# A two-layer decoder trunk on one core: one pool of PSUM banks for the feed-forward, and three changes of order

## The chip, the cores and the metric

The kernel runs on one core of a Trainium2 chip. The core has a matrix engine (TensorE, "PE" in the profile; its weight loads are listed apart as "PEld"), a vector engine (VectorE, "DVE"), a scalar engine (ScalarE, "ACT"), a general engine (GpSimd, "POOL") and a queue that issues transfers (SyncE, "SP"). Each takes its instructions in the order in which they were put into its queue, and waits on semaphores for the others. Matmul results land in PSUM, which has eight banks; a bank holds one tile of 128 x 512 float32. Tiles in PSUM and in SBUF come from pools with a fixed number of buffers, and an instruction that needs a new buffer waits until the last reader of the old one is done.

The metric is the device time of one execution in microseconds, as the median of several runs.

## The reference

The input is x with 1024 tokens of 1024 float32 values. Two layers follow, each with two gated feed-forwards around a mixer:

```python
for layer in range(DEPTH):
    f = swiglu(rmsnorm(h, ffn_pre_g[layer, 0]), ffn_w_gate[layer, 0], ffn_w_up[layer, 0], ffn_w_down[layer, 0])
    h = h + 0.5 * rmsnorm(f, ffn_post_g[layer, 0])
    m = rmsnorm(h, mix_pre_g[layer])
    ...
    h = h + rmsnorm(m, mix_post_g[layer])
    f = swiglu(rmsnorm(h, ffn_pre_g[layer, 1]), ffn_w_gate[layer, 1], ffn_w_up[layer, 1], ffn_w_down[layer, 1])
    h = h + 0.5 * rmsnorm(f, ffn_post_g[layer, 1])
```

`swiglu(x, wg, wu, wd)` is `(silu(x @ wg) * (x @ wu)) @ wd`, with 1024 inputs and 1408 (11 x 128) hidden columns. The mixer of the first layer is differential attention beside gated linear attention, that of the second stick-breaking attention; the change leaves both alone, except that their first projections follow a feed-forward. So there are four feed-forwards, here called l0 f0, l0 f1, l1 f0 and l1 f1.

## The kernel before, in words

All products are made with operands split into two parts, high and low, so that one product of float32 precision is three matmuls (`mm3`, L210 to L212: high by high, high by low, low by high). A split costs one ACT cast (the high part, L200 or L259) and one DVE subtraction (the low part, L201 or L260). The scaled splits of transposed inputs are at L203 and L204. Tokens are worked on in two halves of 512, each of four token tiles of 128.

**Gate and up** (`gu`, L273) are one level of a Strassen-Winograd scheme over token half, half of the input columns, and gate or up. A first loop over the 11 column tiles makes the gate's product of the first token half in a single bank `pa`: a first product over four k tiles (12 matmuls), a copy of it by ACT (L323, kept for later), a second product of 12 matmuls accumulated into the same bank, and the silu of that (L325). After column tile 2 the rows of the second token half are transposed (`make_raw`, L250), and with column tiles 3 to 6 DVE forms the sums that the scheme needs (`combos`, L305 to L314). A second loop over the column tiles makes the rest in the banks `pb`, `pc` and `pd` (60 matmuls a tile), with differences of weights on POOL (L343 to L346).

**Down** (`down_strassen`, L512) is the same scheme over token half, half of the first ten k tiles, and column half; the eleventh k tile is added as it is. Each product has four accumulators, one for each token tile: `da` (two products and the last k tile, 11 x 4 x 3 = 132 matmuls), `db` (60), `dc` (132), `de` (12) and `dd` (60, then a second use of 72). A product is ordered by `product` (L559): for each k tile all four token tiles, and only in the last k tile one token tile after the other. `gained` (L581, L582) reads an accumulator, squares it on ACT (L578) and multiplies it by a gain on DVE. Between the two uses of dd stand the reading of the first (L636), the norm and residual of the first token half (`epilogue`, L446 to L460) and the transposes of its normalised rows for the next stage (`make_x`, L192). After the second use come L644, the norm and residual of the second half, and, at the end of the kernel, the output.

**Buffers.** While a feed-forward runs, PSUM is divided by `open_ffn_psum` (L57) into six banks for accumulators (`acc`) and two for transposes (`tp`). Raw weights have four buffers (`rp`), split weights six (`wp`), one for each k tile of a down product; split token operands have eight (`hp`).

**Behind the feed-forward.** After l0 f0 and l1 f0 the mixer's `first_proj` (L708) projects the first token half for two column tiles (48 matmuls, `pps`), then transposes the second half's rows (`xps`) and projects them, and then closes the feed-forward's pools. After l0 f1 the next `gu` follows.

**What sets the order.** The code states a program order, but instructions are put into the engines' queues by a planner that simulates the engines with its own durations and takes, at each moment, the first instruction in program order that it believes ready. So the queues interleave work of several steps: transposes stand between matmuls of dd, and splits of weights between steps of the norm. Once a queue is made it is fixed; where the chip is slower than the planner thought, an engine waits at the instruction in front.

**Start.** Four row tiles of x are loaded and normalised (`normed`, L181 to L183); `make_x` transposes them column tile by column tile, four transposes to a bank, and splits each. A small transpose (`gps`, L98) brings the gains into columns and takes a bank of `tp`.

Of the kernel before, what the change touches and what calls it, by code (L numbers as in the profile page):

```python
# [19 lines left out]
P = 128  # L20
# [14 lines left out]

class Trunk:
# [20 lines left out]
    def open_ffn_psum(self):  # L57
        self.fctx = ExitStack()
        self.acc = self.dyn(self.fctx, "acc", 6, space=PSUM)
        self.tp = self.dyn(self.fctx, "tp", 2, space=PSUM)  # L60

    def open_fo(self):
        """row buffers of the norms"""
        self.foctx = ExitStack()
        self.fp = self.dyn(self.foctx, "fp", 4, side="right")
        self.hctx = ExitStack()
        self.hrow = self.dyn(self.hctx, "hrow", HB, side="right")

    def open_mix(self, cx, z, t, po):
        """PSUM banks of the mixers; the accumulators of the rest (self.mctx) may outlive the others"""  # L70
# [33 lines left out]
    def mixer_consts(self):  # L104
# [7 lines left out]
        # additive masks, rows q, columns k: NEG where k > q (incl) or k >= q (strict)  # L112
# [9 lines left out]
        # level masks: source row s in the even half of the block of target column t  # L122
# [13 lines left out]
        # lambda of the differential attention, on every partition  # L136
# [20 lines left out]
        # twice: the gate's first factor arrives in two parts, 16 rows each  # L157
# [85 lines left out]
    def make_raw(self, xns, gname, gi, pool):  # L243
        """gained, transposed k tiles, not split"""
# [28 lines left out]
    def gu(self, cx, wg, wu, A, xn1, gname, gi):  # L273
        """A: split k tiles of the first token half; xn1: rows of the second half.
        Returns per column tile, per token half [P, TB] = silu(gate) * up."""
# [23 lines left out]
        def combos(j):  # L299
            # S1 = A21 + A22, S3 = A11 - A21, S2 = S1 - A11, S4 = A12 - S2 (S3, then S4 in A21's place)  # L300
# [15 lines left out]
        ph = []  # L316
        for c in range(NF):
# [6 lines left out]
            self.quarter(ps, w1, A[4:8], False, True)  # L324
            nc.scalar.activation(out=h[0], in_=ps, func=AF.Silu)  # L325
# [3 lines left out]
            if 3 <= c <= 6:  # L329
                combos(c - 3)  # L330
        S[4] = [self.split(R[j], self.xp) for j in range(4)]
# [5 lines left out]
        for c in range(NF):  # L337
# [4 lines left out]
            # T1 = B12 - B11, T2 = B22 - T1, T3 = B22 - B12, T4 = B21 - T2  # L342
# [32 lines left out]
    def down_step(self, w, f0, H, f, KT, accs):  # L375
        """first column half, one K tile, all token tiles"""
# [7 lines left out]
    def down(self, w, H, pg, order=None, prep=None, mid=None, begun=None):  # L384
        """begun: accumulators of the first column half that hold all but the last K tile"""
# [38 lines left out]
    def wp_tag(self):  # L424
        class _W:
            def tile(_, shape, dt, name, tag):
                return self.wp.tile(shape, dt, name=name, tag="w")
        return _W()

# [1 line left out]
    def epilogue(self, tb, fo, ss, half, hsrc, hdst, last):  # L431
        """fo: rows [P, D], or pairs of halves"""
# [68 lines left out]
    # ---- down projection of both token halves: one level of Strassen-Winograd over  # L501
    # (token half, half of the first 2 * KH k tiles, column half); the last k tile is added as it is ----
    def down_sums(self, ph, j):
        """S1 = A21 + A22, S3 = A11 - A21 (in A21's place) of k tile j"""
# [7 lines left out]
    def down_strassen(self, w, ph, pg, hsrc, hdst, nxt):  # L512
# [10 lines left out]
        def raw(j, k=None, cols=None):  # L523
            """[P, 2, TB]: both column halves of k tile j, or a column half of the two k tiles j, k"""
# [13 lines left out]
        # B11 = (j, 0), B12 = (j, 1), B21 = (j + KH, 0), B22 = (j + KH, 1)  # L538
# [727 lines left out]
```

## Time and profile before

| | |
|---|---|
| median of three runs | 2570.22 us (2561.74 to 2572.24) |
| profiled execution | span 2559.7 us; no time of its own beside the span is listed, and the three runs lie 2.0 to 12.5 us above it |
| PE busy | 2452.2 us, 96% |
| DVE, ACT, POOL busy | 1724.8, 1071.6, 665.6 us |
| granted PE clock, mean | 0.987 |
| l0 f0: gate and up / down | 18.4 to 249.7 / 250.0 to 370.5 us |

In the profile's timeline a row holds the start in us from the span's start, the duration in us, the engine, the line, the operation, the tile written and the tiles read, the shapes, the count, and in brackets how long the engine had been idle and what ended that. In tile names the numbers are left out, so `db` is all four accumulators. Durations of matmuls overlap: the next one starts before the last has ended. In a table of stretches each engine has its busy time and, in brackets, its number of instructions. The granted clock is the share of full speed that PE was given.

### The profile page before, as it was taken

The page shows a single profiled execution, that of the slowest core. Times are in us where ns is not written, and L with a number is a line of the kernel's source. Part 1 is how long each engine was busy: PE and PEld are TensorE (multiplying, and loading weights), DVE is VectorE, ACT ScalarE, POOL GpSimd, SP SyncE. Part 2 cuts the span into 40 slices and gives each one's busy share as a digit, 9 for nine tenths or more (in the row PEclk, how much of TensorE's full clock was granted, in tenths as well). Part 3 has the DMA queues.
Part 4 walks back from the last instruction along what each step waited for, and adds up shares of the span by engine and source line. Part 5 has one row for each costly group of instructions (what it writes and reads, how often), then busy time and mean ns, then how long its engine had stood idle before and what let it go on. Part 6 is the DMA issues. An engine that isn't in the chain of part 4 may idle for free.

```text
span 2559.7 us, 32932 instructions
## 1 busy us (share of the span) xinstructions
PE 2452.2 (96%) x12253; PEld 1995.3 (78%) x12253; DVE 1724.8 (67%) x2635; ACT 1071.6 (42%) x2141; POOL 665.6 (26%) x542
## 2 busy tenths in 40 slices
PE   7999999999999999999999998999999999999997
PEld 6787777788777787887777887778888978878776
DVE  6767685754656758667789677845545476676777
ACT  6423454322545646323455234442323344642343
POOL 2445430110000001445424455300000000034543
PEclk9999999999999999999999999999999999999999
DMA  5221551112100254223452215521111034422145
GB/s 176 75 83 65 188 190 49 62 38 75 34 30 34 103 181 123 74 83 115 148 194 83 83 58 181 175 92 35 34 42 34 30 112 163 135 77 79 62 157 188
DMA packets 238841, 251.97 MB, mean 98 GB/s; under 512 B 9860, under 2 KB 186200, under 8 KB 238680
## 3 DMA queue, kind: packets, MB, share of 16 engines
q1 hardware_dynamic: 238680, 249.85, 30.0%
q8 instruction: 97, 1.59, 0.2%
q14 instruction: 64, 0.52, 0.1%
HBM read 215.21 MB, written 34.60 MB: 98 GB/s over the span
## 4 chain that ended last, share of the span: by engine, by line
PE 72%; DVE 15%; issue 4%; DMA 3%; POOL 3%; ACT 3%; SPq 0%; DVEq 0%; POOLq 0%; ACTq 0%
DVE hl L201 4%; PE z L763 4%; PE pps L210 4%; PE pps L212 4%; PE pps L211 4%; PE pd L210 3%; PE pd L211 3%; PE pd L212 3%; PE pc L211 3%; PE pc L212 3%; PE pc L210 3%; DMA rawd<-in_ffn_w_down_dram 2%; PE vps L210 2%; PE vps L211 2%; PE vps L212 2%
## 5 line engine op out<-in xcount | busy, mean ns | idle before, releaser
L172 POOL TENSOR_TENSOR rs<-ms,nhalf 128x1 f32<-128x1 f32 (+1 forms) x136 | 98.6, 732 | 1064.1 <-DVE ms L170 1007.5
L259 ACT CAST wq<-rawt 128x512 fp32r<-128x512 f32 x264 | 163.5, 622 | 340.0 <-PE pc L212 167.2
L260 DVE TENSOR_TENSOR wq<-rawt,wq 128x512 fp32r<-128x512 f32 x264 | 227.7, 866 | 46.6 <-ACT wq L259 41.0
L201 DVE TENSOR_TENSOR hl<-rawd,hl 128x512 fp32r<-128x512 f32 x200 | 162.5, 815 | 106.9 <-ACT hl L200 106.6
L200 ACT CAST hl<-rawd 128x512 fp32r<-128x512 f32 x200 | 123.6, 621 | 223.5 <-issue 60.4
L210 PE MATMUL pps<-hl,wh 128*128 128x512 f32 x512 | 208.3, 408 | 1.1 <-ACT hl L203 1.1
L212 PE MATMUL pps<-hl,wl 128*128 128x512 f32 x512 | 204.1, 399 | 0.0
L211 PE MATMUL pps<-hl,wh 128*128 128x512 f32 x512 | 204.0, 399 | 0.0
L343 POOL TENSOR_TENSOR rawt<-rawt 128x512 f32<-128x512 f32 x44 | 66.5, 1512 | 406.4 <-DMA rawt<-in_ffn_w_up_dram 243.2
L210 PE MATMUL pa<-hl,wq 128*128 128x512 f32 x352 | 140.9, 408 | 12.3 <-ACT ph L323 12.0
L210 PE MATMUL pd<-hl,wq 128*128 128x512 f32 x352 | 140.2, 398 | 10.7 <-DVE c L357 10.7
L210 PE MATMUL vps<-vh,hl 128*128 128x256 f32 x512 | 146.9, 287 | 0.0
L212 PE MATMUL vps<-vh,hl 128*128 128x256 f32 x512 | 145.0, 283 | 0.0
L211 PE MATMUL vps<-vl,hl 128*128 128x256 f32 x512 | 144.8, 283 | 0.0
L780 DVE COPY att<-tps 128x512 f32<-128x512 f32 (+2 forms) x96 | 56.3, 586 | 129.6 <-PE tps L778 129.0
L763 PE MATMUL z<-k,q 128*128 128x512 f32 (+5 forms) x444 | 139.9, 396 | 1.8 <-ACT b L796 1.0
L210 PE MATMUL pc<-hl,wq 128*128 128x512 f32 x352 | 137.7, 391 | 3.6 <-ACT hl L200 3.2
L212 PE MATMUL pa<-hl,wq 128*128 128x512 f32 x352 | 138.9, 397 | 1.6 <-DVE wq L260 1.6
L211 PE MATMUL pa<-hl,wq 128*128 128x512 f32 x352 | 140.2, 398 | 0.0
L211 PE MATMUL pd<-hl,wq 128*128 128x512 f32 x352 | 140.1, 398 | 0.0
L212 PE MATMUL pd<-hl,wq 128*128 128x512 f32 x352 | 139.7, 397 | 0.0
L212 PE MATMUL pc<-hl,wq 128*128 128x512 f32 x352 | 138.3, 393 | 0.0
(280 smaller groups left out, 6725.4 us busy)
## 6 DMA issues: line engine op xcount, KB each, us to landing
rawt<-in_ffn_w_gate_dram SPq DMA_DIRECT2D x88, 512.0 KB, 3.7
rawd<-in_ffn_w_down_dram SPq DMA_DIRECT2D x60, 512.0 KB, 3.6
rawd<-in_ffn_w_down_dram SPq DMA_DIRECT2D x116, 256.0 KB, 2.6
rawt<-in_ffn_w_up_dram SPq DMA_DIRECT2D x44, 512.0 KB, 3.8
hres<-h SPq DMA_DIRECT2D x40, 512.0 KB, 2.9
h<-hres SPq DMA_DIRECT2D x40, 512.0 KB, 5.0
rawt<-in_hyb_w_in_dram SPq DMA_DIRECT2D x16, 512.0 KB, 3.9
rawt<-in_sb_w_qkv_dram SPq DMA_DIRECT2D x16, 512.0 KB, 3.8
```

The costliest lines, as they stand in the source:

```text
L172: nc.gpsimd.tensor_tensor(out=rs, in0=ms, in1=self.nhalf.to_broadcast([P, n]) if n > 1 else self.nhalf, op=ALU.pow)
L200: nc.scalar.copy(out=t[:, 0], in_=src)
L201: nc.vector.tensor_tensor(out=t[:, 1], in0=src, in1=t[:, 0].bitcast(F32), op=ALU.subtract)
L210: nc.tensor.matmul(ps, lhsT=ah, rhs=bh, start=first, stop=False, skip_group_check=more)
L211: nc.tensor.matmul(ps, lhsT=ah, rhs=bl, start=False, stop=False, skip_group_check=more)
L212: nc.tensor.matmul(ps, lhsT=al, rhs=bh, start=False, stop=last, skip_group_check=more)
L259: nc.scalar.copy(out=w[:, 0], in_=src)
L260: nc.vector.tensor_tensor(out=w[:, 1], in0=src, in1=w[:, 0].bitcast(F32), op=ALU.subtract)
L343: gt(out=b11, in0=b12, in1=b11, op=ALU.subtract)
L763: nc.tensor.matmul(z[:, :wide], lhsT=lhs[:, i * P:(i + 1) * P], rhs=rhs[:, c0:c0 + wide], start=j == 0, stop=j == len(passes) - 1 and not ...
L780: (nc.scalar.copy if j0 else nc.vector.tensor_copy)(out=t[:, :n], in_=ps[:, :n])
```

## The change

Four things change in the feed-forward; no arithmetic does.

1. PSUM is one pool of eight banks, from which accumulators and transposes take alike.
2. In the first loop of `gu` the second product of a column tile is issued after the first product of the next column tile (`a12`).
3. `product` takes the last k tile as a part of the same call (`more`), so its operands are split with the others before the matmuls; and the second use of dd gets `tail=KH + 1` = 6, which makes the order "for each token tile all six k tiles" in place of "for each k tile all four token tiles". For the other products the order of matmuls stays as it was.
4. The first transposes of the kernel (`make_first_x`) run token tile by token tile into eight banks, and the splits follow.

```diff
+class Tagged:
+    def __init__(self, pool, tag):
+        self.pool, self.tag = pool, tag
+
+    def tile(self, shape, dtype, name, tag=None):
+        return self.pool().tile(shape, dtype, name=name, tag=self.tag)
...
     def open_ffn_psum(self):
         self.fctx = ExitStack()
-        self.acc = self.dyn(self.fctx, "acc", 6, space=PSUM)
-        self.tp = self.dyn(self.fctx, "tp", 2, space=PSUM)
+        self.acc = self.dyn(self.fctx, "acc", 8, space=PSUM)
+        self.tp = Tagged(lambda: self.acc, "acc")
...
+    def make_first_x(self, xns, gname, gi, pool):
+        ps = [self.tp.tile([P, TB], F32, name="xps") for k in range(KD)]
+        for t in range(NTT):
+            for k in range(KD):
+                self.nc.tensor.transpose(ps[k][:, t * P:(t + 1) * P], xns[t][:, k * P:(k + 1) * P], self.ident)
+        return [self.split(ps[k], pool, scale=self.col(gname, gi * KD + k)) for k in range(KD)]
...
+        second = []
+
+        def a12():
+            ps, w1, h = second.pop()
+            self.quarter(ps, w1, A[4:8], False, True)
+            nc.scalar.activation(out=h[0], in_=ps, func=AF.Silu)
+
         for c in range(NF):
...
             self.quarter(ps, w0, A[0:4], True, True)
             nc.scalar.copy(out=h[1], in_=ps)
-            self.quarter(ps, w1, A[4:8], False, True)
-            nc.scalar.activation(out=h[0], in_=ps, func=AF.Silu)
+            if second:
+                a12()
+            second.append((ps, w1, h))
             ph.append(h)
...
+        a12()
         S[4] = [self.split(R[j], self.xp) for j in range(4)]
...
-        def product(accs, a, b, start, ks=range(KH)):
+        def product(accs, a, b, start, ks=range(KH), more=None, tail=TAIL):
             As, Bs = [], []
-            for j in ks:
-                As.append(self.split(a(j), self.hp))
-                Bs.append(self.split(b(j), wp))
+            for a, b, ks in [(a, b, ks)] + ([more] if more else []):
+                for j in ks:
+                    As.append(self.split(a(j), self.hp))
+                    Bs.append(self.split(b(j), wp))
             n = len(As)
-            m = max(0, n - TAIL)
+            m = max(0, n - tail)
...
-        product(pa, A(0, 1), lambda j: half(j + KH, 0), False)
-        product(pa, *last_k(0, 0))
+        product(pa, A(0, 1), lambda j: half(j + KH, 0), False, more=last_k(0, 0))
...
-        product(pd, A(1, 1), t4, False)
-        product(pd, *last_k(1, 0))
+        product(pd, A(1, 1), t4, False, more=last_k(1, 0), tail=KH + 1)
...
-        x0 = self.make_x(self.xn0, "ffn_pre_g", 0, self.xp)
+        x0 = self.make_first_x(self.xn0, "ffn_pre_g", 0, self.xp)
```

More of the change, by code (lines that the diff above doesn't have):

```diff
@@ L424, in wp_tag @@
     def wp_tag(self):
[L425 to L428, printed above, removed]
+        return Tagged(lambda: self.wp, "w")
     def epilogue(self, tb, fo, ss, half, hsrc, hdst, last):
@@ L584, in down_strassen @@
         A = lambda tb, kh: (lambda j: ph[j + kh * KH][tb])
-        last_k = lambda tb, c: (lambda j: ph[NF - 1][tb], lambda j: half(NF - 1, c), False, [0])
+        last_k = lambda tb, c: (lambda j: ph[NF - 1][tb], lambda j: half(NF - 1, c), [0])
         s1 = lambda j: self.s1[j]
@@ L617, in down_strassen @@
             tt(out=c22[t], in0=pc[t], in1=u2[t], op=ALU.add)
-        product(pc, A(0, 1), lambda j: half(j + KH, 1), False)
-        product(pc, *last_k(0, 1))
+        product(pc, A(0, 1), lambda j: half(j + KH, 1), False, more=last_k(0, 1))
         for t in range(NTT):
@@ L625, in down_strassen @@
         pe = new("de")
-        a, b, _, ks = last_k(1, 1)
+        a, b, ks = last_k(1, 1)
         product(pe, a, b, True, ks)
```

## The prediction

> **What bounds the kernel now.** I read the engine totals and the chain of waits first, then the waits of TensorE, then stretches and timelines around each long wait.
>
> ```profile
> PE 2452.2 (96%) x12253; PEld 1995.3 (78%) x12253; DVE 1724.8 (67%) x2635; ACT 1071.6 (42%) x2141; POOL 665.6 (26%) x542
> ...
> PE 72%; DVE 15%; issue 4%; DMA 3%; POOL 3%; ACT 3%; SPq 0%; DVEq 0%; POOLq 0%; ACTq 0%
> ```
>
> TensorE is the bound almost everywhere: time can only come from its idle stretches and from the ends of the kernel, where it has nothing to do. Its longest waits (total, times, longest):
>
> ```profile
> PE db L210 <- DVE fo L582: 15.6, 4, 4.6
> PE pa L210 <- ACT ph L323: 12.0, 5, 4.0
> ...
> PE xps L192 <- DVE ms L170: 7.1, 13, 1.5
> PE xps L192 <- DVE xn L183: 6.5, 4, 2.4
> PE dd L210 <- DVE fo L636: 3.6, 7, 1.4
> ...
> PE dd L210 <- DVE c L629: 1.5, 3, 0.6
> ```
>
> The change touches all six. The next view is a table of stretches; its columns are width, busy time and count of PE, of PE's weight loads, of DVE, ACT and POOL, then PE's granted clock, DMA share and rate. First the db product in the four feed-forwards, from its first matmul to the first one of dc, and for comparison dc with de, which runs without a wait.
>
> ```profile
> 279.90:300.00 20.10, 15.49 (x62) 12.33 (x60) 15.21 (x20) 9.26 (x20) 8.57 (x6) 0.92 0.47 167
> 1225.10:1245.10 20.00, 16.43 (x61) 13.05 (x60) 14.12 (x18) 9.27 (x20) 8.05 (x6) 0.83 0.40 143
> 1573.70:1593.20 19.50, 15.47 (x61) 12.27 (x60) 14.76 (x18) 9.27 (x20) 8.46 (x6) 0.91 0.41 151
> 2464.70:2482.00 17.30, 13.93 (x62) 11.19 (x60) 14.94 (x19) 9.27 (x20) 7.83 (x6) 1.00 0.45 158
> 300.00:329.90 29.90, 29.90 (x133) 24.77 (x132) 20.46 (x31) 12.91 (x23) 8.94 (x7) 1.00 0.42 141
> ```
>
> A matmul of 512 columns, issued without a gap, costs 29.90 / 132 = 0.2265 us (the printed mean of 0.39 us overlaps the next one). The granted clock under 1.00 shows a second cost of idling: stretches of half speed behind the wait. The next two rows are such a pair in the first feed-forward: an idle stretch, then eight matmuls in 3.50 us, 1.7 us more than 8 x 0.2265.
>
> ```profile
> 74.00:78.40 4.40, 0.44 (x2) 0.01 (x1) 4.40 (x9) 2.77 (x6) 0.00 (x0) 1.00 0.00 0
> 78.40:81.90 3.50, 3.50 (x8) 2.75 (x9) 3.50 (x7) 1.09 (x2) 0.00 (x0) 0.51 0.52 150
> 332.60:371.00 38.40, 35.50 (x163) 26.89 (x162) 34.95 (x58) 21.14 (x43) 10.74 (x11) 1.00 0.62 200
> 382.00:395.00 13.00, 7.06 (x25) 4.74 (x24) 7.84 (x13) 5.66 (x10) 3.71 (x5) 0.64 0.21 84
> ...
> 2546.20:2559.70 13.50, 0.00 (x0) 0.00 (x0) 9.10 (x22) 1.67 (x6) 2.29 (x4) 0.63 0.42 157
> ```
>
> The other three are the two products of dd in the first feed-forward, the start of the mixer behind it, and the end of the kernel after the last matmul. They are used below.
>
> **The change part by part.** No instruction of compute is added or taken away; what changes is which bank a tile gets and the order asked for.
>
> *Eight banks: db.* The timeline of the first db product:
>
> ```profile
> 280.58 0.39 PE L210 MATMUL db<-hl 128*128 128x512 f32 x1
> ...
> 282.16 1.54 DVE L201 TENSOR_TENSOR hl<-t,hl 128x512 fp32r<-128x512 f32 x1
> ...
> 285.29 1.87 DVE L582 TENSOR_TENSOR fo<-da,pg 128x512 f32<-128x512 f32 x3
> ...
> 286.02 0.50 PE L210 MATMUL db<-hl 128*128 128x512 f32 x1 [4.61 <-DVE fo L582]
> ```
>
> Token tiles 0 and 1 of db get the two banks that da leaves; tile 2 waits until DVE has read da at L582. With eight banks db has four of its own. The four stretches hold 20.10 + 20.00 + 19.50 + 17.30 = 76.9 us; 4 x 60 matmuls at 0.2265 are 54.4; the difference, half clock included, is 22.5. What is late next are the split weights of db: its fifth and last ends at 282.16 + 1.54 = 283.7, and db wants it at 279.9 + 4 x 12 x 0.2265 = 290.8. So nothing takes the wait's place: I take **22**, with 17.9 as lower end (the busy DVE as bound, below) and 22.5 as upper.
>
> *The later second gate product.* The order of the queues at the long wait for L323:
>
> ```profile
> 70.22 1.74 POOL L345 TENSOR_TENSOR rawt<-rawt 128x512 f32<-128x512 f32 x1
> ...
> 70.72 1.78 DVE L201 TENSOR_TENSOR hl<-s,hl 128x512 fp32r<-128x512 f32 x1
> ...
> 74.13 0.68 DVE L305 TENSOR_TENSOR s<-xr 128x512 f32<-128x512 f32 x1
> ...
> 74.84 0.62 ACT L200 CAST hl<-s 128x512 fp32r<-128x512 f32 x1 [5.67 <-DVE s L305]
> ...
> 77.77 0.58 ACT L323 COPY ph<-pa 128x512 f32<-128x512 f32 x1
> ...
> 78.40 0.73 PE L210 MATMUL pa<-hl,wq 128*128 128x512 f32 x1 [3.96 <-ACT ph L323]
> ```
>
> DVE's element-wise rows take 1.78 instead of 0.68 us while POOL works, ACT stands behind DVE, and the copy of the first product stands behind that in ACT's queue. The second product of the tile cannot accumulate into the bank before the copy. In the new order the second product of the tile before, 12 matmuls or 2.7 us, lies between: a wait of 3.96 becomes about 1.2. Three long waits lose 2.7 each, 8.2; the two short ones (12.0 less three of about 3.8) some 0.6; three half-clock stretches of 1.7 go if the rest is short, 5.1. Sum 13.9; I take **13**. Upper end 17 (12.0 + 5.1); lower end -3, if the queue's next item, a weight split by the same busy DVE, is what PE then waits for, and the split held a tile longer in the six weight slots costs a little (0.7 per feed-forward).
>
> *The last down product tile by tile.* dd is used twice; its second use now includes the last k tile and asks for token tile 0 over all six k tiles, then tile 1, and so on. Three effects:
>
> (a) The waits for L636 and L629 (5.1 in all) fall away but for the first tile's: **+3** (0 to 5).
>
> (b) Tile 0 needs all six operand pairs at once. In the first feed-forward the second use began at 347.28, and the last pairs came late from DVE:
>
> ```profile
> 347.28 0.47 PE L210 MATMUL dd<-hl 128*128 128x512 f32 x1 [0.39 <-DVE fo L636]
> ...
> 350.84 0.50 PE L210 MATMUL dd<-hl 128*128 128x512 f32 x1 [0.34 <-DVE fo L636]
> ...
> 356.37 0.68 DVE L201 TENSOR_TENSOR hl<-rawd,hl 128x512 fp32r<-128x512 f32 x1
> ...
> 356.53 0.41 PE L192 MATMUL xps<-ident,fo 128*128 128x128 f32 x2 [1.08 <-DVE ms L170]
> ...
> 360.08 0.68 DVE L201 TENSOR_TENSOR hl<-rawd,hl 128x512 fp32r<-128x512 f32 x1
> ```
>
> The fifth pair is there at 357.05, the sixth at 360.76. Taken strictly, tile 0 would leave PE idle from 350 to 357 and again to 360.8, some 9 us after the transposes that fit in. Not strictly, as the transposes placed between dd's matmuls in these rows show that the planner fills, tiles 1 to 3 use the ready pairs and nothing is lost. I take 1 us per feed-forward, **-4** (-32 to 0), nearer the filling that the rows show.
>
> (c) The chains behind the product start earlier. Two lead into a mixer, where PE has 48 matmuls (11 us) left and then waits for normalised rows; with the L170 and L183 waits (7.1 + 6.5) and half clock (0.64 in 382:395) that is some 14.5 in all. A tile's chain costs DVE about 4 us (add, gain, two residual halves, normalisation), and in 332.6:371 DVE is busy 34.95 of 38.40: room for about one tile of three. So 4 per mixer, **+8** (0 to 14.5). Behind the feed-forward that leads into another one: **+1** (0 to 2.5). At the end of the kernel 13.5 us pass after the last matmul, with DVE work for all four tiles in them:
>
> ```profile
> 2537.91 0.68 DVE L201 TENSOR_TENSOR hl<-rawd,hl 128x512 fp32r<-128x512 f32 x1
> ...
> 2544.15 2.05 DVE L644 TENSOR_TENSOR fo<-dd,u 128x512 f32<-128x512 f32 x3 [5.56 <-PE dd L212]
> ```
>
> DVE has 5.56 us of free time before it, and that is the most that can move: **+4** (2 to 5.5).
>
> *The first transposes token tile by token tile.* Rows of the start:
>
> ```profile
> 10.28 0.69 PE L192 MATMUL xps<-ident,fx 128*128 128x128 f32 x2
> ...
> 12.01 0.75 DVE L183 TENSOR_SCALAR fx<-fx,rs 128x1024 f32<-128x1024 f32 x1 [0.45 <-POOL rs L172]
> ...
> 13.58 1.11 PE L192 MATMUL xps<-ident,fx 128*128 128x128 f32 x4 [0.29 <-DVE gcol L101]
> ...
> 18.41 0.78 PE L210 MATMUL pa<-hl,wq 128*128 128x512 f32 x1
> ...
> 20.83 0.60 PE L192 MATMUL xps<-ident,fx 128*128 128x128 f32 x4
> ```
>
> At 18.41 half of the 32 transposes are done; the rest come between matmuls. Now 24 can run before the fourth row tile is there (12.76). At the early pace, 1.11 for four of which the last overlaps (0.21 each), 32 from 10.3 end at 17.1: 1.3 earlier, with 16 transposes more behind them, which later cost about 0.09 each, 1.4. Together 2.7; I take **+2.5** (0 to 4.5; -1 if the eight banks, one of which holds the gains' transpose, block the first product).
>
> [...]
>
> **Sum:** 22 + 13 + 3 - 4 + 8 + 1 + 4 + 2.5 = 49.5 us less. The profiled execution has a span of 2559.7; the three runs take 2561.7 to 2572.2, so 2 to 12.5 lie around it. Against the median: 2570.2 - 49.5 = 2520.7, say **2521**. About 0.5% (13 us) is what a measurement can tell from no change.
>
> **The rivals.**
>
> *The waits move to DVE* (for: DVE is busy 15.21 of 20.10 us in db's stretch and 4.40 of 4.40 before L323; against: the weights of db are split seven microseconds ahead). Then db lasts as long as DVE's work in it, saving 4.9 + 5.9 + 4.7 + 2.4 = 17.9, and the gate's 13 is nil: 32.4 in all, **2538**.
>
> *The common pool does not deliver* (for: eight transposed tiles and four dd accumulators do not fit eight banks if these are handed out in turn; against: each bank is free again after one ACT and one DVE read, 0.69 + 0.75). Half of the transposed tiles would wait for dd, 4 x (0.69 + 0.75) or 5.8 us later, at three transitions: 17 lost, **2538** too.
>
> *The starved last product* is the slower side: PE takes the order strictly. 9 idle, 1.7 at half clock, and 3 for the next stage's weights, since all six slots are held into the last token tile: 13.7 in three feed-forwards. The last one ends at 2546.2, so its second use begins 72 x 0.2265 before, at 2529.9; five pairs take 3.4, and the sixth is there at 2538.6: 5.3 idle and 1.7. That is 48; if the sixth load comes late too, by a load, a subtraction and a split (5.2), 69. The gains outside (22 + 13 + 3 + 2.5 = 40.5) are used up at 10.1 per feed-forward; it is measurably slower from 13.3. Midway: 2570 + 18 = **2588**. For: the rows of (b). Against: the transposes between.
>
> [...]
>
> *Everything is hidden*: db 22.5, gate 17, dd 4, no starving, mixers 14.5, 2.5, end 5.5, start 2.5: 68.5, **2502**.
>
> **How the numbers follow.** Forecast 0.45, DVE 0.22, pool 0.10, all hidden 0.18, starved 0.05. The forecast's own bounds, with terms that miss independently, are about 2507 to 2540. The range takes in the two cases of 2538 and their spread and nearly all of the hidden one: 2497 to 2550, leaving out the starved case and tails. Faster by over 0.5% in nearly all but the starved case; with something for a planner that reorders every queue: 0.88 faster, 0.08 within, 0.04 slower.
>
> **What would show it.** db's stretch at 13.6 to 14 us with clock 1.00 and no wait for L582; the wait for L323 under 1.5; L644's first row several microseconds ahead of the last matmul and fewer than 10 us behind it; the first pa near 17; dd's second use no longer than 24 us. Wrong: waits of dd for L201, of pa for L260, or of pps and pa for weights behind dd.

## The result and the profile after

The changed kernel takes **2507.86 us** in the median of 4 runs (2504.94 to 2509.04), beside 2570.07 us for the kernel before (4 runs, 2561.74 to 2572.24): a ratio of 0.9771, 95% interval 0.9755 to 0.9786. The forecast was 2521 in a range of 2497 to 2550. The profiled execution took 2509.04 us with a span of 2507.3; that of before, with its span of 2559.7, fits the run of 2561.74. So the sum of 49.5 us is to be held against 52.4 between two profiled executions, and 62 between the medians. One run of one kernel below took 2680.57 us at a granted clock of 0.848, where that kernel's other three runs have 0.996 and 0.997; it is left out of that kernel's median.

The page of the changed kernel: engine totals, then the shares of the chain of waits.

```profile
PE 2430.2 (97%) x12253; PEld 1995.7 (80%) x12253; DVE 1733.3 (69%) x2635; ACT 1069.0 (43%) x2143; POOL 671.2 (27%) x542
...
PE 82%; DVE 10%; issue 3%; POOL 2%; ACT 2%; DMA 2%; DVEq 0%; SPq 0%; POOLq 0%; ACTq 0%
```

The number of matmuls is the same. PE's busy time fell by 22 us with the same instructions, so that they ran faster (mean granted clock 0.987 before, 0.994 after); the other 30 us were idle time. In the chain PE's share rose from 72 to 82%, DVE's fell from 15 to 10%. The waits of PE after (total, times, longest):

```profile
PE pd L228 <- DVE c L385: 10.7, 4, 2.7
...
PE xps L210 <- DVE xn L193: 4.3, 5, 1.7
PE pa L230 <- DVE wq L278: 4.1, 2, 3.2
PE dd L228 <- DVE fo L662: 3.9, 4, 1.3
...
PE pa L228 <- DVE hl L222: 3.4, 1, 3.4
...
PE xps L210 <- DVE ms L180: 2.8, 9, 0.5
PE dd L229 <- DVE hl L219: 2.7, 3, 0.9
PE xps L201 <- DVE gcol L111: 2.7, 1, 2.7
...
PE dd L228 <- ACT hl L218: 1.3, 1, 1.3
...
PE pa L228 <- ACT ph L349: 0.7, 1, 0.7
```

The two waits at the head of before's list are gone: 15.6 us of db for the reading of da to nothing, 12.0 us of `pa` for the copy (now L349) to 0.7. New, or longer than before, are `pa` for a weight split (L278; 1.6 us before), dd for late operands (L219, L218), and two waits at the start of the kernel (L111, L222). The longest, `pd` for L385, was in the kernel before too; it lies in the up loops and the prediction did not look at it. The stretches that answer to those of before: db in the four feed-forwards, dc with de, dd, 13 us in the first mixer from 11.3 us behind its first product on (as 382:395 before), and the end.

```profile
276.90:290.50 13.60, 13.60 (x62) 11.27 (x61) 13.46 (x16) 9.08 (x20) 8.50 (x6) 1.00 0.59 210
1202.00:1215.60 13.60, 13.60 (x62) 11.26 (x61) 11.76 (x15) 8.50 (x20) 8.52 (x6) 1.00 0.56 192
1544.90:1558.50 13.60, 13.60 (x62) 11.27 (x61) 13.46 (x16) 9.07 (x20) 7.63 (x6) 1.00 0.53 182
2418.70:2432.30 13.60, 13.60 (x62) 11.27 (x61) 13.46 (x18) 8.74 (x20) 7.30 (x5) 1.00 0.50 174
290.50:320.40 29.90, 29.90 (x133) 24.77 (x132) 21.66 (x34) 13.05 (x23) 9.08 (x7) 1.00 0.45 150
323.10:361.40 38.30, 35.49 (x165) 27.37 (x164) 35.55 (x62) 20.88 (x43) 10.68 (x11) 1.00 0.55 174
372.70:385.70 13.00, 11.04 (x62) 9.18 (x63) 9.89 (x15) 7.67 (x14) 3.67 (x4) 1.00 0.32 105
2497.70:2507.30 9.60, 0.00 (x0) 0.00 (x0) 4.77 (x11) 0.72 (x2) 1.10 (x2) 0.63 0.42 158
```

db is 13.60 us four times, with PE busy in all of it. The stretch in the mixer has 62 matmuls and transposes at full clock where before's had 25 at 0.64. Behind the last matmul DVE has 4.77 us of work left, not 9.10.

For the whole ledger I cut both traces at the first matmul of each stage; a "gate" runs from the first `pa` to the first `pc`, an "up" from there to the first da, a mixer from its first `pps` to the first `dps` of the output projection. Sums over the feed-forwards, in us:

| stage | before | after | difference |
|---|---|---|---|
| start of the span to the first product | 18.4 | 22.7 | +4.3 |
| four gate loops (77.4, 73.2, 71.7, 72.9) | 295.2 | 276.2 (70.1, 66.1, 73.9, 66.1) | -19.0 |
| four up loops | 617.4 | 615.7 | -1.7 |
| db | 77.0 | 54.4 | -22.6 |
| dd (the last one to its last matmul) | 147.1 | 148.2 | +1.1 |
| mixers (474.0, 427.2) | 901.2 | 888.0 (466.3, 421.7) | -13.2 |
| output projections (123.1, 116.1) | 239.2 | 241.1 (124.0, 117.1) | +1.9 |
| behind the last matmul's start | 14.0 | 10.0 | -4.0 |

That is 53.2 less; the products not listed give back the rest, to 52.4.

### The profile page after: what moved, and what is told of

Read it like the earlier page. It is cut to its first block, busy times and chain, and to the rows that moved or that the text cites. A ratio compares the mean times of both kernels' runs of the same rounds, so it can differ in the third digit from the quotient of the medians.

```text
span 2507.3 us, 32918 instructions
## 1 busy us (share of the span) xinstructions
PE 2430.2 (97%) x12253; PEld 1995.7 (80%) x12253; DVE 1733.3 (69%) x2635; ACT 1069.0 (43%) x2143; POOL 671.2 (27%) x542
## 4 chain that ended last, share of the span: by engine, by line
PE 82%; DVE 10%; issue 3%; POOL 2%; ACT 2%; DMA 2%; DVEq 0%; SPq 0%; POOLq 0%; ACTq 0%
PE z L788 4%; PE pps L228 4%; PE pps L230 4%; PE pps L229 4%; PE pd L228 3%; PE pd L230 3%; PE pd L229 3%; PE pa L230 3%; PE pa L228 3%; PE pa L229 3%; PE pc L229 3%; PE pc L230 3%; PE pc L228 3%; PE vps L228 3%; PE po L831 2%
## 5 line engine op out<-in xcount | busy, mean ns | idle before, releaser
L182 POOL TENSOR_TENSOR rs<-ms,nhalf 128x1 f32<-128x1 f32 (+1 forms) x136 | 100.2, 743 | 1046.1 <-DVE ms L180 950.4
L278 DVE TENSOR_TENSOR wq<-rawt,wq 128x512 fp32r<-128x512 f32 x264 | 242.8, 924 | 22.6 <-ACT wq L277 16.7
L219 DVE TENSOR_TENSOR hl<-rawd,hl 128x512 fp32r<-128x512 f32 x200 | 166.2, 834 | 86.6 <-ACT hl L218 86.3
L218 ACT CAST hl<-rawd 128x512 fp32r<-128x512 f32 x200 | 123.7, 621 | 208.5 <-issue 46.7
L371 POOL TENSOR_TENSOR rawt<-rawt 128x512 f32<-128x512 f32 x44 | 72.0, 1636 | 395.9 <-DMA rawt<-in_ffn_w_up_dram 184.9
L228 PE MATMUL pd<-hl,wq 128*128 128x512 f32 x352 | 139.9, 397 | 10.7 <-DVE c L385 10.7
L228 PE MATMUL pa<-hl,wq 128*128 128x512 f32 x352 | 138.7, 394 | 4.1 <-DVE hl L222 3.4
L230 PE MATMUL pa<-hl,wq 128*128 128x512 f32 x352 | 138.1, 393 | 4.1 <-DVE wq L278 4.1
L228 PE MATMUL pc<-hl,wq 128*128 128x512 f32 x352 | 137.6, 391 | 3.1 <-ACT hl L218 3.1
L230 PE MATMUL pc<-hl,wq 128*128 128x512 f32 x352 | 138.3, 393 | 0.0
L229 PE MATMUL pc<-hl,wq 128*128 128x512 f32 x352 | 138.3, 393 | 0.0
```

The source lines that it names most:

```text
L182: nc.gpsimd.tensor_tensor(out=rs, in0=ms, in1=self.nhalf.to_broadcast([P, n]) if n > 1 else self.nhalf, op=ALU.pow)
L218: nc.scalar.copy(out=t[:, 0], in_=src)
L219: nc.vector.tensor_tensor(out=t[:, 1], in0=src, in1=t[:, 0].bitcast(F32), op=ALU.subtract)
L228: nc.tensor.matmul(ps, lhsT=ah, rhs=bh, start=first, stop=False, skip_group_check=more)
L229: nc.tensor.matmul(ps, lhsT=ah, rhs=bl, start=False, stop=False, skip_group_check=more)
L230: nc.tensor.matmul(ps, lhsT=al, rhs=bh, start=False, stop=last, skip_group_check=more)
```

## The experiments

Each edit makes the planner put all queues together anew, so small differences far from an edit are not the edit's own. All times are medians beside the kernel before on the same chip (2562.96 to 2566.72 us there); "span" is the profiled execution's.

**One part taken out, or one part alone.** The eight banks alone, in the kernel before:

```diff
-        self.acc = self.dyn(self.fctx, "acc", 6, space=PSUM)
-        self.tp = self.dyn(self.fctx, "tp", 2, space=PSUM)
+        self.acc = self.dyn(self.fctx, "acc", 8, space=PSUM)
+        self.tp = Tagged(lambda: self.acc, "acc")
```

> The kernel before with one change: PSUM of the feed-forward as one pool of eight banks. Theory A (the wait of db for L582 is a lack of banks and nothing else, and the shorter starts of the mixers come from the token-tile order of the last product): the four db stretches go from 76.9 to 54.4 us, nothing else moves by more than 2, span 2559.7 - 22.5 = 2537. Rival B (more banks for transposes shorten the mixers' starts too, 7.7 + 5.6 us in the changed kernel): span about 2524. Both would allow the output projections, whose pools are opened by the same function, to be 1 us longer each.

Measured: 2532.22 us, ratio 0.9877 (0.9860 to 0.9893), span 2532.9. db is 13.6 four times, so this part carries its 22.6 alone. The mixers shorten too, by 5.3 and 4.3 us, without any tile order, as the rival had it. But the third gate loop gets longer, from 71.7 to 77.3, which neither case foresaw, so the span lies between the two expected. In the list of PE's waits:

```profile
PE xps L258 <- DVE xn L191: 7.3, 1, 7.3
```

With banks free, the planner put the transposes of the second token half early into PE's queue, where they waited 7.3 us for their normalised rows, with the gate's matmuls behind them.

The changed kernel without the tile order:

```diff
-        product(pd, A(1, 1), t4, False, more=last_k(1, 0), tail=KH + 1)
+        product(pd, A(1, 1), t4, False, more=last_k(1, 0))
```

> The changed kernel with the second use of dd in the old order (all four token tiles for each k tile). Theory A (the token-tile order is what shortened the mixers' starts by 13.3 us and the end by 3.9, and it costs 2.2 in the gate loop behind the feed-forward that leads into another): span 2507.3 + 13.3 + 3.9 - 2.2 - 0.6 = 2522. Rival B (the eight banks shortened the mixers' starts): the end alone is lost and the gate loop gets its 2.2 back, span about 2509.

Measured: 2512.41 us, 0.9801 (0.9786 to 0.9815), span 2511.2. The end takes 14.0 us again; the mixers lose only 0.8 and 1.6. The third gate loop does not get back the 2.2 us that both cases expected: it takes 75.1, beside 73.9 in the changed kernel. The kernel before with the tile order alone (`more` and `tail=KH + 1` as in the change):

> The kernel before (six and two banks) with only the last product changed: the last k tile in the same call, and the second use of dd token tile by token tile. Theory A (with two banks for transposes an earlier chain does not help the mixers' starts; the order gives the end of the kernel and costs about 1 us in each dd): end 10 instead of 14, mixers within 2 each, span 2559.7 - 4 to -1, about 2556. Rival B (as predicted, the chain behind dd sets the mixers' starts, and the order shortens them by 4 each whatever the banks): span about 2548.

Measured: 2563.77 us, 0.9994 (0.9979 to 1.0009), span 2564.7. The end is 4.1 us shorter (9.9) and the mixers 2.9 and 1.6, but the third gate loop is 7.6 longer (79.3). The db stretches, whose order the edit leaves alone, take 81.3 instead of 77.0. In the whole this part moves nothing that can be measured.

The changed kernel without the deferred product, where `a12()` follows each first product at once:

```diff
-            if second:
-                a12()
             second.append((ps, w1, h))
+            a12()
...
-        a12()
```

> The changed kernel with the second gate product of a tile issued straight after its first. Theory A (the deferred product covers ACT's late copy): the waits of pa for L349 come back, about 3.9 us with 1.7 of half clock in three feed-forwards, span 2507.3 + 17 = 2524. Rival B (these waits ended because the planner made another order with eight banks): no such wait, span 2507 within 3.

Measured: 2535.39 us, 0.9893 (0.9879 to 0.9908), span 2532.8. The gate loops are 76.1, 72.7, 80.8 and 74.0, together 27.4 more than in the changed kernel (17 were expected for the whole kernel), and the wait for the copy is back:

```profile
PE pa L228 <- ACT ph L349: 13.4, 6, 3.6
```

The deferred product alone in the kernel before:

> The kernel before with only the second gate product issued after the first of the next tile. Theory A (the deferral works by itself: a gate loop behind finished inputs runs at 66 us instead of 73): gate loops of l0 f1 and l1 f1 66, about 6 less in the other two, span 2559.7 - 26 = 2534. Rival B (it needs the eight banks, since two pa banks live at a time beside pb to pd): gate loops above 69, span 2545 or more.

Measured: 2544.19 us, 0.9918 (0.9894 to 0.9943), span 2542.9. Gate loops 73.8, 66.7, 69.6, 66.7: 18.4 less than before. The other two gave 3.6 and 2.1 where 6 each were expected, and db takes 81.8 here, so the span lies 9 us above the expectation. The second and fourth are near what their work takes: 276 matmuls at 0.2265 us are 62.5, and 32 transposes at some 0.11 (in the changed kernel's third gate loop they start 0.109 us apart from 1309.27 on) are 3.5, together 66.0 by this estimate.

The changed kernel with the first transposes as before (`make_x`):

```diff
-        x0 = self.make_first_x(self.xn0, "ffn_pre_g", 0, self.xp)
+        x0 = self.make_x(self.xn0, "ffn_pre_g", 0, self.xp)
```

> The changed kernel with the first transposes column tile by column tile, as before. Theory A (the token-tile order of the first transposes is a loss here: one bank is held by the gains' transpose, PE waits 2.7 us for it and the first product starts at 22.7 instead of 18.4): first product at about 18, span 2507.3 - 5 = 2502. Rival B (the later start is made up in the first gate loop, where DVE and ACT and not PE set the pace): first product at 18, but span 2507 within 1.5.

Measured: **2500.55 us**, 0.9762 (0.9747 to 0.9776), span 2498.8: 8.5 us less than the changed kernel's span. The first product starts at 18.6 instead of 22.7, and the first gate loop takes 68.1 instead of 70.1. So this part of the change costs 6.1 us at the start of the kernel. That the whole time falls with it is less sure: the ratios to the kernel before, 0.9762 here and 0.9771 for the changed kernel, are not apart.

**Why the first transposes lose.** Two causes were to be told apart: the bank that the gains' transpose holds, and DVE's queue. The changed kernel's start, from the timelines of PE and of DVE (start, duration, engine, line, operation, tiles, count, idle time before and what ended it):

```profile
14.04 5.18 PE L201 MATMUL xps<-ident,fx 128*128 128x128 f32 x25 [2.68 <-DVE gcol L111]
22.66 0.79 PE L228 MATMUL pa<-hl,wq 128*128 128x512 f32 x1 [3.43 <-DVE hl L222]
```

```profile
20.54 0.20 DVE L144 CAST lm<-lmf 128x64 int32<-128x64 f32 x1 [1.69 <-POOL lmf L141]
20.65 1.29 DVE L278 TENSOR_TENSOR wq<-rawt,wq 128x512 fp32r<-128x512 f32 x2
21.85 2.72 DVE L222 SCALAR_TENSOR_TENSOR hl<-xps,gcol,hl 128x512 fp32r<-128x512 f32 x4
```

The 25 transposes wait for the bank until 14.04 and are through at 19.22. Then DVE waits at the last of seven casts of masks (one for each entry of `LEVELS`), which POOL is still making for a mixer that starts 340 us later; the weight split and the first split of x stand behind it. The first experiment gets round the bank: the eighth column tile is transposed last.

```diff
-        for t in range(NTT):
-            for k in range(KD):
+        for t, k in [(t, k) for t in range(NTT) for k in range(KD - 1)] + [(t, KD - 1) for t in range(NTT)]:
```

> The changed kernel with the eighth column tile of the first transposes put behind the other seven, so that the bank held by the gains' transpose stops nothing. Theory A (the held bank makes the late start): 28 transposes run as the row tiles come, first product at about 20, span 2507.3 - 3 = 2504. Rival B (DVE's first splits stand in its queue behind casts of masks that wait for POOL, until 20.65): first product still at 22 to 23, span 2507 within 1.5.

Measured: 2507.89 us, 0.9778 (0.9754 to 0.9801), span 2504.0. The rows of PE and DVE:

```profile
10.71 5.98 PE L200 MATMUL xps<-ident,fx 128*128 128x128 f32 x32
22.39 0.80 PE L227 MATMUL pa<-hl,wq 128*128 128x512 f32 x1 [5.70 <-DVE hl L221]
```

```profile
12.21 0.75 DVE L193 TENSOR_SCALAR fx<-fx,rs 128x1024 f32<-128x1024 f32 x1 [0.45 <-POOL rs L182]
...
20.27 0.20 DVE L144 CAST lm<-lmf 128x64 int32<-128x64 f32 x1 [1.69 <-POOL lmf L141]
20.38 1.29 DVE L277 TENSOR_TENSOR wq<-rawt,wq 128x512 fp32r<-128x512 f32 x2
21.59 2.72 DVE L221 SCALAR_TENSOR_TENSOR hl<-xps,gcol,hl 128x512 fp32r<-128x512 f32 x4
```

All 32 transposes are done at 16.7, and the product starts no earlier than 22.39. With the casts where they were, the bank was not what set the start. Then, on top of this, the casts go to POOL:

```diff
-            nc.vector.tensor_copy(out=mi, in_=m)
+            nc.gpsimd.tensor_copy(out=mi, in_=m)
```

> The changed kernel with two edits: the gains' transpose finds a free bank (the first transposes make the eighth column tile last), and the six casts of the masks lm run on GpSimd instead of VectorE. If the first product starts at 22.7 us because the second halves of the splits stand behind these casts in VectorE's queue, while the casts wait for GpSimd's affine_selects, the first product starts between 16.5 and 19 us and the span is 2497 to 2502 us, median about 2503. If the cold transposes and the arrival of the last row tile set the start, it stays at 22 to 23 us and the span at 2504 to 2508, as with the first edit alone (22.4 us, 2504.0).

Measured: 2500.63 us, 0.9756 (0.9739 to 0.9774), span 2498.6.

```profile
15.76 1.42 PE L200 MATMUL xps<-ident,fx 128*128 128x128 f32 x11 [1.17 <-DVE fx L193]
18.02 0.50 PE L227 MATMUL pa<-hl,wq 128*128 128x512 f32 x1 [0.84 <-DVE hl L221]
```

```profile
14.95 0.75 DVE L193 TENSOR_SCALAR fx<-fx,rs 128x1024 f32<-128x1024 f32 x1 [1.70 <-POOL rs L182]
...
15.98 1.32 DVE L277 TENSOR_TENSOR wq<-rawt,wq 128x512 fp32r<-128x512 f32 x2
17.23 5.34 DVE L221 SCALAR_TENSOR_TENSOR hl<-xps,gcol,hl 128x512 fp32r<-128x512 f32 x8
```

The weight split moves from 20.38 to 15.98 and the first product from 22.39 to 18.02, by the casts alone. DVE's queue was the cause. Even so this kernel is no faster than the one with the old order (2498.6 and 2498.8). But that does not settle what the new order is worth, for the edit has a price of its own: POOL also makes a factor of each row tile's normalisation (`rs`, L182), and with the casts in its queue the last row tile is normalised at 15.7 instead of 13.0 (the L193 rows), so the first splits of x, eight of 0.67 us on DVE, cannot begin before. The new order with the casts on neither of these queues was not run.

**The third gate loop.** It is the one behind another feed-forward, and the only one that the change made longer (71.7 to 73.9). If its transposes wait for late rows, they can be asked for a column tile later (with the first transposes as before):

```diff
-            if c == 2:
+            if c == 3:
...
-            if 3 <= c <= 6:
-                combos(c - 3)
+            if 4 <= c <= 7:
+                combos(c - 4)
```

> The changed kernel with the old first transposes (as old_first_x) and with the second token half's transposes and sums one column tile later in the gate loop. Theory A (the gate loop of l1 f0 loses its 7 us because PE meets the transposes of rows that are not yet normalised): that loop 67 instead of 72.8, the others unchanged, span 2498.8 - 5 = 2494. Rival B (the loss is DVE's, which has the norm's chain and the weight splits at once; later sums then come too late for the second loop): that loop still above 71 or the second loops longer, span 2498 or more.

Measured: 2507.14 us in three runs, 0.9772 (0.9744 to 0.9799), span 2503.2. The third gate loop is 72.5 beside 72.8 with the first transposes as before, and the up loops get a new wait, of `pc` for L383, 5.5 us in four. So it is not the transposes. The wait is at the front of the loop; the changed kernel, PE and DVE:

```profile
1294.01 0.50 PE L230 MATMUL pa<-hl,wq 128*128 128x512 f32 x1 [3.19 <-DVE wq L278]
```

```profile
1288.63 0.69 DVE L278 TENSOR_TENSOR wq<-rawt,wq 128x512 fp32r<-128x512 f32 x1
...
1290.49 2.74 DVE L480 SCALAR_TENSOR_TENSOR h<-fo,rs,h 128x512 f32<-128x512 f32 x4
...
1293.27 0.69 DVE L278 TENSOR_TENSOR wq<-rawt,wq 128x512 fp32r<-128x512 f32 x1
```

Between two weight splits of the new loop DVE does the residual sums of the last token tiles (L480), and PE waits for the second. The order of the rows shows this; no run here took the norm's chain away from DVE.

**What the banks give to the mixers.** Beside the kernel with old first transposes, six banks and two again:

```diff
-        self.acc = self.dyn(self.fctx, "acc", 8, space=PSUM)
-        self.tp = Tagged(lambda: self.acc, "acc")
+        self.acc = self.dyn(self.fctx, "acc", 6, space=PSUM)
+        self.tp = self.dyn(self.fctx, "tp", 2, space=PSUM)
```

> The changed kernel with the first transposes as before, and with the banks parted again into 6 for accumulators and 2 for transposes in the feed-forward; the deferred gate product and the tile order stay. Beside the same kernel with eight banks in one pool (span 2498.8): the db stretches go back from 13.6 to about 20 us each, +25; the output projections give 1.9 back. If the eight banks also made the mixers' starts shorter, these grow by 4 to 9 us and the span is 2526 to 2531, median about 2530. If the tile order made them shorter, as predicted before the result, they stay and the span is about 2522, median about 2524.

Measured: 2540.24 us, 0.9912 (0.9890 to 0.9934), span 2537.8, which is 39.0 more: db 24.9, mixers 4.7 and 3.4, gate loops 5.4, output projections 1.8 less. The mixers answer to the banks, as in the kernel with the banks alone. The gate loops, and 2.0 us in the up loops, I had not put into the expectation, so the span came out 7 us above it. How the banks act is seen where the second token half enters the first mixer. The kernel before, PE and ACT:

```profile
389.16 0.69 PE L192 MATMUL xps<-ident,xn 128*128 128x128 f32 x2 [2.40 <-DVE xn L183]
391.43 1.05 PE L192 MATMUL xps<-ident,xn 128*128 128x128 f32 x4
...
398.73 0.61 PE L192 MATMUL xps<-ident,xn 128*128 128x128 f32 x4
```

```profile
389.67 1.27 ACT L203 ACTIVATE hl<-xps,gcol 128x512 fp32r<-128x512 f32 x2 [4.21 <-PE xps L192]
...
399.38 0.69 ACT L203 ACTIVATE hl<-xps,gcol 128x512 fp32r<-128x512 f32 x1 [0.22 <-PE xps L192]
```

With two banks, only two column tiles could be begun ahead of the last row tile, 6 transposes of 32 (that tile's first transposes start at 389.16); the other six column tiles follow one by one as ACT and DVE hand banks back, and the last split starts at 399.38. The changed kernel:

```profile
373.33 1.72 PE L210 MATMUL xps<-ident,xn 128*128 128x128 f32 x14 [0.84 <-DVE xn L193]
375.44 0.77 PE L210 MATMUL xps<-ident,xn 128*128 128x128 f32 x5 [0.40 <-DVE xn L193]
376.89 1.64 PE L210 MATMUL xps<-ident,xn 128*128 128x128 f32 x13 [0.68 <-DVE xn L193]
```

```profile
377.25 4.74 ACT L221 ACTIVATE hl<-xps,gcol 128x512 fp32r<-128x512 f32 x8 [2.53 <-PE xps L210]
```

19 of 32 transposes are done ahead of the last rows, and all eight splits run as one row of 4.74 us, done 5.1 us after the last rows' first transposes instead of 10.9.

The banks and the tile order do not do the same. Over the first 35 us of each mixer, the waits of `xps` sum to 8.9 us in the kernel before, and the granted clock is 0.85 and 0.90. The tile order alone takes the waits to 4.1, but the clock only to 0.90 and 0.95. The banks alone leave 5.7 us of waits, but the clock is 1.00 in both. The changed kernel has 4.3 and 1.00.

**The wait left in every kernel.** `pd` for L385 and `pc` for a split stand at the end of each up loop, 13.9 us in all. The kernel with old first transposes, DVE:

```profile
231.58 4.05 DVE L219 TENSOR_TENSOR hl<-ph,hl 128x512 fp32r<-128x512 f32 x3
235.55 0.68 DVE L385 TENSOR_TENSOR c<-pd,c 128x512 f32<-128x512 f32 x1
```

Splits for the down product stand ahead of the add that reads `pd`, and PE's next product accumulates into `pd`. In the last column tile the two products get banks of their own:

```diff
+            if c == NF - 1:
+                pc2 = self.acc.tile([P, TB], F32, name="pc2", tag="acc")
+                pd2 = self.acc.tile([P, TB], F32, name="pd2", tag="acc")
+                tt(out=c21, in0=pc, in1=u2, op=ALU.add)
+                self.quarter(pc2, w4, A22, True, True)
+                tt(out=c21, in0=pc2, in1=c21, op=ALU.add)
...
+                tt(out=c12, in0=pd, in1=u2, op=ALU.add)
+                self.quarter(pd2, w3, S[4], True, True)
+                tt(out=c12, in0=pd2, in1=c12, op=ALU.add)
```

> The changed kernel with the first transposes as before, and in the last column tile of the second up loop the two last products get banks of their own, so that TensorE does not wait for VectorE to add the earlier contents; the sums are made by two more adds per block. Beside the same kernel without this edit (span 2498.8): the waits of pd for c (10.7 us) and of pc for hl (3.2 us) lie there. If they are a matter of banks alone, they go, with the stretches at half clock behind them: 12 to 20 us, span 2479 to 2487, median about 2485. If VectorE's backlog of splits for the down products is what is late, the wait moves to the first products of da or db, and the gain is under 4 us, span 2495 to 2499.

Measured: **2489.00 us** (2487.46 to 2492.47), 0.9710 (0.9693 to 0.9728), span 2485.7, the best kernel here. The first up loop without and with the edit:

```profile
86.60:240.80 154.20, 150.74 (x649) 122.69 (x648) 111.73 (x138) 45.48 (x73) 79.78 (x54) 0.99 0.26 74
```

```profile
86.60:235.20 148.60, 148.60 (x649) 121.68 (x648) 107.72 (x135) 44.90 (x72) 74.88 (x51) 1.00 0.26 75
```

All four up loops are 148.6 with no wait, 20.4 us less in sum; 7.3 come back later, most of it in dc with de (0.8 to 1.2 each in three), dd (1.6) and the second mixer (2.5).

Last, on top of this, half of the tile order:

```diff
-        product(pd, A(1, 1), t4, False, more=last_k(1, 0), tail=KH + 1)
+        product(pd, A(1, 1), t4, False, more=last_k(1, 0), tail=3)
```

> The kernel with own banks at the end of the up loops (span 2485.7), and in it the last down product goes token tile by token tile over its last 3 pieces of K instead of all 6. If the order over all 6 pieces costs the third gate loop its 3 to 4 us (73.3 us, beside 69.6 in the kernel with the deferred product alone) because the last token tile's sums, norms and weight splits crowd on VectorE, and costs the waits for late operands in dd (5.4 us in four stages), then half of the order gives back part of both: third gate loop 70 to 72, dd stages 1 to 3 us shorter in sum, the end 10.0 to 12, span 2480 to 2485. If these 3 us come from the schedule of the deferred product and not from the order, the third gate loop stays at 73 to 74 and only the end moves, to 11 to 13: span 2485 to 2489.

Measured: 2489.96 us, 0.9717 (0.9699 to 0.9735), span 2487.0. The third gate loop is 72.0 (from 73.3), the last dd 0.9 shorter, the end 12.1 (from 10.0), and a mixer 1.0 longer. The direction fits the crowding on DVE; the gain expected of it did not come, and 1.3 us of one gate loop settle nothing. Why the deferred product alone has 69.6 there stays open.

## Why the prediction was right, and where not

The time fell inside the range, 13 us below the forecast. That the sum of 49.5 comes so near to 52.4 is luck: two terms were too small, two had the wrong sign, and a cost was missing.

- **db, 22 (17.9 to 22.5).** Right: 22.6, in the changed kernel and with the banks alone. DVE was busy 13.46 of 13.60 us in it and still held nothing up: the split weights were ahead, as worked out.
- **The later gate product, 13 (-3 to 17).** The mechanism was right, the size too small: 19.0 in the ledger, 18.4 alone, 25.5 in the span when it is taken out of the changed kernel. The step that failed is "the second product of the tile before, 12 matmuls or 2.7 us, lies between". By the code two products lie between a copy's bank being filled and its next use: the second of the tile before and the first of the tile after, 24 matmuls or 5.4 us. That covers the longest wait of 4.0 whole, where I left 1.2 of it; what remains is 0.7 us once. The rest was not in the list of waits at all: of the 7.0 us that the second gate loop lost, the long wait (3.61) and the half clock with it (3.41 us at 0.50) are 5.3, and the others are delays of at most 0.2 us between single matmuls, too short to be listed. The loops behind a mixer reach the 66 us that their work takes (66.1 each).
- **(a) and (b), +3 and -4.** Together right: dd +1.1 in the ledger. One by one, not as told: the waits for L636 (L662 now) did not fall (3.6 in seven, 3.9 in four; L629's 1.5 are gone), and late operands cost 2.7 + 1.3 = 4.0, the 4 foreseen. dd's second use takes 23.6 us in the first feed-forward (24 was the bound given).
- **(c) mixers, +8 (0 to 14.5).** 13.2: inside the range, but mostly for another reason. The step that failed is "The chains behind the product start earlier", with 4 for each mixer: that is the tile order, which gives 4.5 in both together when alone and 2.4 when it is taken out last; the eight banks give 9.6 alone and 8.1. The prediction read the waits of `xps` for DVE as late rows, and did not ask how many of the eight column tiles could be transposed ahead of them. It also put all 13.6 us of the two lines into the mixers; 8.6 stand there, and the rest at transposes in the dd stages and at the start.
- **+1 into the next feed-forward.** Wrong in sign: the third gate loop is 2.2 longer. PE waits 3.2 us there for a weight split (`pa` for L278), with a stretch at half clock behind it (0.50 from 1295.30 to 1302.10), as the rival has it in which the waits move to DVE. What puts the split there is open: the loop is longer with the banks alone (77.3) and with the tile order alone (79.3), but no shorter without the tile order (75.1).
- **End, +4 (2 to 5.5).** Right: 4.0 in the changed kernel, 4.1 alone, with DVE's work behind the last matmul down from 9.10 to 4.77.
- **First transposes, +2.5 (-1 to 4.5).** Wrong in sign: 6.1 us lost at the start (4.1 + 2.0). The step that failed took PE's transposes as what sets the first product. That all 32 keep the early 0.21 us, as the term has it, no run shows: with the bank free they start 0.11 apart from 15.4 on. They were done at 16.7 there, near the 17.1 of the sum, but the product started at 22.39: DVE's queue set it, and there the splits had come to stand behind casts that wait for POOL. In the old order the first splits stand between these casts.
- **Not in the sum:** 0.9 to 1.2 us for each output projection, in every kernel with eight banks there and in none without. No row shows an added wait of that size, and the cause was not tried.

The rivals: db did not last as long as DVE; the pool delivers, four db stretches and the mixers show it; PE was not starved: in the first feed-forward the last operand of dd's second use was split at 351.12, and by then PE had begun 40 of the 72 matmuls, where the strict order allows 15. The median lies nearer to "everything is hidden" (2502) than its chance says, and not because everything was hidden: the terms were read in before's fastest run and taken from its median. The profiled run of before is 8.3 us faster than the median of its runs, and that is most of the difference between 52.4 and 62.

## What to carry to other kernels

Ask of a wait for a bank how many tiles could have been ready ahead of the late operand: here the pool of eight gave two to three times as much in the mixers as the tile order from which that gain was expected. Work that has no hurry (masks for a later stage) should not stand in the queue of an engine whose next item starts the kernel; moved to another queue, it can hold up what stands there. And look at the longest wait that a change does not touch: 10.7 us of `pd`, in plain sight in every list, was worth more than two of the four parts of the change, for a bank of its own to each of two products.

## What the runs showed of the hardware

**The pace of the first transposes.** In the kernel that goes round the bank, nothing but transposes has run on PE (after the gains' one) when the first two of these stretches follow each other:

```profile
10.70:15.40 4.70, 4.70 (x23) 4.69 (x23) 2.53 (x10) 1.14 (x2) 2.80 (x10) 1.00 1.00 285
15.40:16.50 1.10, 1.10 (x12) 1.05 (x10) 0.20 (x1) 0.86 (x2) 0.71 (x3) 1.00 1.16 294
...
22.35:25.60 3.25, 3.21 (x8) 2.55 (x9) 3.25 (x6) 0.00 (x0) 0.00 (x0) 0.50 0.81 266
```

Up to 15.4 the transposes start 0.21 us apart (22 in 4.70 us), from then on 0.11 (the other ten in 1.10). In the changed kernel the run of 25 that begins at 14.04 has its starts 0.213 apart up to 18.58 and 0.11 from 18.74 on, 4.6 us into the run and 3.9 us ahead of the first matmul of `pa`. In the kernel before, eight transposes follow the wait of 1.67 us that ends at 16.37, and `pa`'s first matmul starts 2.0 us later; its matmuls start 0.43 apart from 18.99 to 20.27, and the four transposes from 20.83 on 0.11. The prediction took the early 0.21 for all 32; in the two kernels above the pace rose ahead of the first matmul. (The granted clock reads 1.00 in both of the first rows and so does not tell the two paces apart.) The third row follows 5.70 us without work: there the first products run at 0.50. In the kernel with the casts on POOL only 0.84 us without work lie ahead of the first products, and they start 0.23 apart from 18.36 on. What sets these paces, no run here shows.

**The clock beside PE's long waits.** In the kernel before, 12 of the 13 waits of more than 2 us (those at the start left out) have a stretch of 3.4 to 10.2 us at half clock (0.50) with them; the last db, with a wait of 3.37 us, has none, and took 17.30 us at clock 1.00. With the tile order alone the same stretch is:

```profile
2469.90:2489.90 20.00, 16.33 (x61) 12.94 (x60) 14.21 (x18) 9.27 (x20) 8.16 (x6) 0.83 0.40 143
```

The same product, 2.7 us longer, at 0.83. The kernel with old first transposes shows it within one execution: `pd` waits 2.7 us in all four up loops; three have half clock with it (mean clock 0.99) and take 154.2, 154.1 and 153.9 us, the fourth has none (1.00) and takes 152.6. What decides it, no run here shows. Runs of one kernel differ in it too: of the ten with the tile order alone, the fastest (2557.93) has a mean granted clock of 0.989, the slowest (2568.24) of 0.983.
